# Six k-chunks cut 1, 2, 3, 3, 4, 3 in place of 1, 2, 2, 3, 4, 4, late transposes spread out, modulation sums two slots later

## The chip, the cores and the metric

The kernel runs on one core of a Trainium2 chip. The metric is device time in microseconds (us) of one launch. "PE" is the matmul engine, "PEld" its weight load, DVE the vector engine, ACT the scalar engine, POOL GpSimd, and SP the queue that issues nearly all DMAs.

## What is computed

One layer of a bidirectional hybrid encoder on 512 positions of width 2048, all in float32:

```python
mod = silu(c) @ w_ada + b_ada                  # (1, 6144)
shift, scale, gate = split(mod, 3)
h = rms_norm(x, g) * (1 + scale) + shift       # (512, 2048)
proj = h @ w_in                                # (512, 7168): q,k,v,z of 8 attention heads, q,k,v,z of 4 retention heads
y_a = dilated_attention_mixture(q_a, k_a, v_a) # three windows, ALiBi, mixed by their softmax denominators
y_r = bidirectional_retention(q_r, k_r, v_r)
y = concat(y_a * silu(z_a), y_r * silu(z_r))
out = rms_norm(x + gate * (y @ w_out), final_gain)
```

Keeping float32's accuracy, the kernel splits both operands of each large product into a high and a low part and issues three matmuls (`mm3`, L93 to L96: high·high, high·low, low·high).

## The kernel before, in words

The width 2048 is 16 tiles of 128, called k. `h` for a tile needs the modulation of that tile (128 columns of shift and 128 of scale, over all 2048 rows of `w_ada`), and the projection needs `h`. So the kernel starts the projection before all modulation is there. `CHUNKS` (L36) cuts the 16 tiles into six chunks. For each chunk the loop at the end of the first part (`for ci, nk in enumerate(CHUNKS)`) runs 13 units, each 256 columns of `w_in` (q, k, v, z of three pairs of attention heads, q of the fourth). Two units (`persist`) hold their sums in four PSUM banks over all chunks; the other 11 use three banks in turn (pool `psA`, tile `pw`), and after each chunk their partial sums are added into SBUF accumulators on DVE (L973, `acc<-acc,pw`; the first time ACT copies). A unit fills two banks, one half after the other, and a half can only begin when the bank of three halves before has been added. One unit per chunk, the last in order, is left in PSUM and goes on into the next chunk.

A unit of a chunk is cut into items of at most two k tiles: a chunk of 1 or 2 has 13 items, one of 3 has 26 (two tiles, then one), one of 4 has 26. An item has a load (SP), a conversion (`conv`: the high part on ACT, L178; the low part on DVE, L183) and its matmuls. `feed` keeps loads 8 items and conversions 2 items ahead of the matmuls, so matmuls run ten slots behind the feed. Chunks of 1 or 2 tiles share loads between units (`shared_conv`, 512 KB for two neighbouring units); larger ones load each unit by itself.

An `agenda` puts side work into the slots of the feed. `plan` spreads the pieces for the next chunk evenly over this chunk's items: `ada_pieces` gives loads of `w_ada` (SP, L230, tile `araw`, three buffers), products that accumulate 16 row tiles (L241 on DVE, `aacc<-araw,ct,aacc`; the first of the 16 is L237 on ACT), then `sums` (L271: PE transposes the accumulators into the one bank of pool `psM`; ACT reduces them with `junk`, L276; DVE adds the bias, L278 to L280), then `h_pieces` (ACT L195 and L200; DVE L209, `hl<-ht,hh`). For the first chunk `sums` is the short form at L255 to L261.

Side work too: `last_rows`, the transposes of the last 128 positions of x (L378, `psx`, through the same `psM` bank; DVE or ACT copies them out, L389). The four pieces stand in feed slots 10, 11, 12 and 13. In the second half of the last chunk the attention of finished heads runs between the items (`run_queue`, pieces separated by `None`, one group per item), and goes on through the units after it.

Which instruction of an engine stands where is decided by a scheduler from this program order.

Of the kernel before, what the change touches and what calls it, by code (L numbers as in the profile page):

```python
# [32 lines left out]
OFF_QA, OFF_KA, OFF_VA, OFF_ZA = 0, 1024, 2048, 3072  # L33
OFF_QR, OFF_KR, OFF_VR, OFF_ZR = 4096, 4608, 5120, 6144
UC = 256
CHUNKS = [1, 2, 2, 3, 4, 4]  # L36
N_PERSIST = 2
ADA_SPAN = 0.65
TAB_SPAN = 16
WARM = 4, 1, 1  # L40
FIRST_W = OFF_KA + UC
LAG = 3
RAW, RAW1, WB, LOOK, LEAD, LEAD0, LEAD1, EB, YB = 3, 3, 3, 2, 4, 2, 8, 1, 22


# [9 lines left out]
def trunk_kernel(ctx, tc, x, c, norm_gain, w_ada, b_ada, w_in, w_out, dec_f, dec_b, final_gain, out):  # L55
# [46 lines left out]

    groups = [range(sum(CHUNKS[:i]), sum(CHUNKS[: i + 1])) for i in range(len(CHUNKS))]
    xt_tiles = {i: hp.tile([P, len(g), S], F32, tag=f"g{i}", name=f"xT{i}") for i, g in enumerate(groups) if i}
# [108 lines left out]
    def h_pieces(k0, nk):  # L213
        return [(lambda f=f, k=k: f(k, nk, k0)) for f in (make_h, make_hl) for k in range(k0, k0 + nk)]

    def ada_pieces(k0, nk):
# [6 lines left out]
        def load(kr):  # L223
            raw = aap.tile([P, 2048], F32, tag="araw", name="araw", bufs=AR)
            rv = raw[:, : npc * 2 * n].rearrange("p (a b f) -> p a b f", a=npc, b=2)
            src = wa[kr * P : (kr + npc) * P, 0 : 2 * D].rearrange(
                "(a p) (b f) -> p a b f", p=P, b=2
            )[:, :, :, k0 * P : k0 * P + n]
            for b in range(2):
                nc.sync.dma_start(rv[:, :, b], src[:, :, b])  # L230
            raws[kr] = rv

        def add(kr):
            rv = raws[kr]
            for a in range(npc):
                if kr + a == 0:
                    first = nc.scalar.activation(acc[:, :, :n], rv[:, a], AF.Copy, scale=ct[:, 0:1])  # L237
                    if k0 in (1, 3):
                        after(first, marks["hh"])
                else:  # L240
                    ins = nc.vector.scalar_tensor_tensor(  # L241
                        acc[:, :, :n], rv[:, a], ct[:, kr + a : kr + a + 1], acc[:, :, :n],
                        op0=ALU.mult, op1=ALU.add,
                    )
                    if k0 in (1, 3) and kr + a == 1:
                        after(ins, marks["hl"])
# [37 lines left out]
        def step(i):  # L284
            if i >= AR:
                add(krs[i - AR])
            if i < len(krs):
                load(krs[i])

        return (  # L290
            [(lambda i=i: step(i)) for i in range(len(krs) + AR)]
            + [sums]
            + h_pieces(k0, nk)
        )
# [182 lines left out]
    def last_rows(b):  # L477
        if b == 1:
            v = xn[3][:, 1024:D]
            after(nc.vector.tensor_scalar_mul(v, v, rsx[:, 3:4]), marks["sc"])  # L480
        turned(3, b, True)
        evacuated(3, b, dve if b else act, True)

    late = [lambda b=b: last_rows(b) for b in range(4)]
# [429 lines left out]
    k0 = 0  # L914
    agenda = {}
    fed = 0

    for i, f in enumerate(late):
        agenda.setdefault(LEAD1 + LOOK + i, []).append(f)

    def plan(fs, start, span):
        for i, f in enumerate(fs):
            agenda.setdefault(start + (i * span) // len(fs), []).append(f)
# [14 lines left out]

    for ci, nk in enumerate(CHUNKS):
        lastc = ci == len(CHUNKS) - 1  # L940
        early["on"] = ci < len(CHUNKS) - 2
        items = []
        order = ORDER
        if (len(CHUNKS) - 1 - ci) % 2:
            order = order[::-1]
# [48 lines left out]
        if not lastc:  # L994
            n2 = CHUNKS[ci + 1]
            nxt = []
            for i in range(0, n2, 4):
                nxt += ada_pieces(k0 + nk + i, min(4, n2 - i))
            before_last = ci == len(CHUNKS) - 2
            span = int(len(items) * ADA_SPAN) if before_last else len(items)  # L1000
            plan(nxt, fed + LAG, span)
            if before_last:
                agenda.setdefault(fed + LAG + span, []).append(open_wk)
        if ci == 0:
# [358 lines left out]
```

## Time and profile before

| | |
|---|---|
| median of 3 runs | 942.23 us (941.79 to 944.12) |
| the profiled execution, its own time | 941.63 us |
| its span, first to last instruction | 939.9 us |
| granted TensorE clock over the span | 0.997 |
| PE / DVE / ACT busy over the span | 98% / 66% / 40% |

A matmul's row in the trace overlaps the next one's, since the engine is pipelined; how fast PE goes is read from the distance between starts, or from how many matmuls a stretch holds. Seen from PE, the first chunk begins at 25 us, the second at about 47, the third at about 86, the fourth at about 129, the fifth at about 185 and the last at about 258 us.

### The profile page before, as it was taken

What the parts mean: (1) busy time and instruction counts of PE and PEld (TensorE: products, weight loads), DVE (VectorE), ACT (ScalarE), POOL (GpSimd) and SP (SyncE); (2) the same over time, 40 slices, a digit from 0 to 9 for tenths busy, and PEclk for the clock granted to TensorE, in tenths of its full rate; (3) what the DMA queues carried; (4) which work ended last, traced back from release to release, by engine and by line L of the source; (5) the groups of instructions that cost most, each with busy time, mean ns of one, the idle gap of its engine ahead of it and who ended that gap; (6) DMA issues with size and microseconds to landing.
All of it is one profiled execution on the core that took longest, in us unless ns stands there. A gap on an engine that the chain in (4) does not pass through costs nothing.

```text
span 939.9 us, 14334 instructions
## 1 busy us (share of the span) xinstructions
PE 919.8 (98%) x5578; PEld 806.7 (86%) x5578; DVE 619.6 (66%) x1096; ACT 379.0 (40%) x747; POOL 12.5 (1%) x25
## 2 busy tenths in 40 slices
PE   8999899999999999999999999999999999999996
PEld 5787688888988888988998899998899988888896
DVE  4899999949557786666675565745644382547554
ACT  4843426253244655444443233422333372324321
POOL 2000000000000000000000000000000000000001
PEclk9999999999999999999999999999999999999998
DMA  9997798533332222214444534445523148244305
GB/s 329 352 311 245 253 318 298 175 94 113 107 96 68 68 68 68 68 46 135 146 146 141 179 107 154 140 126 165 163 64 113 59 160 297 90 125 143 109 5 180
DMA packets 110244, 141.50 MB, mean 151 GB/s; under 512 B 5800, under 2 KB 81496, under 8 KB 109792
## 3 DMA queue, kind: packets, MB, share of 16 engines
q1 hardware_dynamic: 109072, 137.27, 45.3%
q10 hardware_dynamic: 1008, 3.28, 0.9%
q8 instruction: 44, 0.72, 0.3%
q14 instruction: 24, 0.20, 0.1%
q0 software_dynamic: 96, 0.03, 0.0%
HBM read 136.36 MB, written 4.20 MB: 150 GB/s over the span
## 4 chain that ended last, share of the span: by engine, by line
PE 85%; DVE 7%; DMA 4%; issue 2%; ACT 1%; POOL 0%; SPq 0%; POOLq 0%; DVEq 0%; ACTq 0%
PE pp L96 24%; PE pp L94 12%; PE pw L96 12%; PE po L96 12%; PE pw L94 6%; PE po L94 6%; PE op L96 3%; DVE aacc L241 3%; DMA araw<-in_w_ada_dram 3%; PE sp L96 2%; PE op L94 2%; DVE acc L973 1%; PE tp L797 1%; DVE w L183 1%; DMA raw<-in_w_ada_dram 1%
## 5 line engine op out<-in xcount | busy, mean ns | idle before, releaser
L183 DVE TENSOR_TENSOR w<-raw,w 128x512 fp32r<-128x512 f32 (+1 forms) x288 | 193.1, 672 | 216.4 <-ACT w L178 214.0
L178 ACT CAST w<-raw 128x512 fp32r<-128x512 f32 (+1 forms) x289 | 174.8, 607 | 399.0 <-PE pp L96 187.6
L94 PE MATMUL pp<-w,hh 128*128 128x256 f32 x576 | 160.1, 278 | 0.0
L96 PE MATMUL pp<-w,hh 128*128 128x256 f32 x576 | 159.6, 277 | 0.0
L96 PE MATMUL pp<-w,hl 128*128 128x256 f32 x576 | 159.6, 277 | 0.0
L94 PEld LDWEIGHTS pp<-w,hh 128*128 128x128 f32 x576 | 108.2, 188 | 1.0 <-issue 0.3
L96 PEld LDWEIGHTS pp<-w,hh 128*128 128x128 f32 x576 | 108.2, 188 | 0.9
L96 PEld LDWEIGHTS pp<-w,hl 128*128 128x128 f32 x576 | 108.4, 188 | 0.0
L94 PE MATMUL pw<-hh,w 128*128 128x512 f32 x256 | 101.9, 399 | 4.3 <-DVE acc L973 3.5
L96 PE MATMUL pw<-hh,w 128*128 128x512 f32 x256 | 100.2, 392 | 0.4 <-DVE w L183 0.4
L94 PE MATMUL pp<-hh,w 128*128 128x512 f32 x256 | 99.7, 392 | 0.4 <-DVE kl L697 0.4
L96 PE MATMUL pp<-hl,w 128*128 128x512 f32 x256 | 100.0, 391 | 0.0
L96 PE MATMUL pp<-hh,w 128*128 128x512 f32 x256 | 99.9, 390 | 0.0
L96 PE MATMUL pw<-hl,w 128*128 128x512 f32 x256 | 99.6, 390 | 0.0
L96 PE MATMUL po<-w,yh 128*128 128x512 f32 (+1 forms) x252 | 91.0, 361 | 0.0
L94 PE MATMUL po<-w,yh 128*128 128x512 f32 (+1 forms) x252 | 91.0, 361 | 0.0
L96 PE MATMUL po<-w,yl 128*128 128x512 f32 (+1 forms) x252 | 91.0, 361 | 0.0
L241 DVE SCALAR_TENSOR_TENSOR aacc<-araw,ct,aacc 128x512 f32<-128x512 f32 (+2 forms) x75 | 76.0, 1014 | 5.8 <-ACT aacc L237 2.6
L973 DVE TENSOR_TENSOR acc<-acc,pw 128x512 f32<-128x512 f32 x100 | 66.5, 681 | 5.2 <-PE pw L96 4.8
L94 PEld LDWEIGHTS pw<-hh,w 128*128 128x128 f32 x256 | 48.0, 188 | 19.8 <-DVE acc L973 7.5
L96 PEld LDWEIGHTS pw<-hh,w 128*128 128x128 f32 x256 | 48.1, 188 | 10.9 <-DVE w L183 0.8
L94 PEld LDWEIGHTS pp<-hh,w 128*128 128x128 f32 x256 | 48.0, 188 | 10.8 <-DVE kl L697 0.8
(235 smaller groups left out, 1558.2 us busy)
## 6 DMA issues: line engine op xcount, KB each, us to landing
raw<-in_w_in_dram SPq DMA_DIRECT2D x94, 512.0 KB, 3.7
araw<-in_w_ada_dram SPq DMA_DIRECT2D x48, 512.0 KB, 6.2
graw<-in_w_ada_dram SPq DMA_DIRECT2D x64, 256.0 KB, 3.1
raw<-in_w_out_dram SPq DMA_DIRECT2D x32, 512.0 KB, 3.7
raw<-in_w_in_dram SPq DMA_DIRECT2D x16, 384.0 KB, 3.8
araw<-in_w_ada_dram SPq DMA_DIRECT2D x16, 384.0 KB, 4.0
res<-in_x_dram SPq DMA_DIRECT2D x16, 256.0 KB, 6.6
raw<-in_w_in_dram SPq DMA_DIRECT2D x11, 256.0 KB, 5.6
```

Of the source, the lines that this page charges most:

```text
L94: nc.tensor.matmul(o, lh, rh, start=start, stop=False, skip_group_check=True)
L96: nc.tensor.matmul(o, a, b, start=False, stop=stop and b is (rl if swap else rh), skip_group_check=True)
L178: c1 = nc.scalar.copy(dh, src)
L183: c2 = nc.vector.tensor_tensor(dl, src, f32(dh), op=ALU.subtract)
L241: ins = nc.vector.scalar_tensor_tensor(acc[:, :, :n], rv[:, a], ct[:, kr + a : kr + a + 1], acc[:, :, :n], op0=ALU.mult, op1=ALU.add,)
L797: nc.tensor.transpose(tp_[:, j * P : (j + 1) * P], pt[:, j * P : (j + 1) * P], ident)
L973: nc.vector.tensor_tensor(accs[u][i], accs[u][i], ps[i], op=ALU.add)
```

## The change

```diff
--- before.py
+++ after.py
@@ -33,13 +33,15 @@
 OFF_QA, OFF_KA, OFF_VA, OFF_ZA = 0, 1024, 2048, 3072
 OFF_QR, OFF_KR, OFF_VR, OFF_ZR = 4096, 4608, 5120, 6144
 UC = 256
-CHUNKS = [1, 2, 2, 3, 4, 4]
+CHUNKS = [1, 2, 3, 3, 4, 3]
 N_PERSIST = 2
 ADA_SPAN = 0.65
 TAB_SPAN = 16
 WARM = 4, 1, 1
 FIRST_W = OFF_KA + UC
 LAG = 3
+LATER = 2
+LATE = 10, 19, 23, 26
 RAW, RAW1, WB, LOOK, LEAD, LEAD0, LEAD1, EB, YB = 3, 3, 3, 2, 4, 2, 8, 1, 22
 
 
@@ -289,6 +291,7 @@
 
         return (
             [(lambda i=i: step(i)) for i in range(len(krs) + AR)]
+            + [lambda: None] * (LATER if k0 > 1 else 0)
             + [sums]
             + h_pieces(k0, nk)
         )
@@ -915,8 +918,8 @@
     agenda = {}
     fed = 0
 
-    for i, f in enumerate(late):
-        agenda.setdefault(LEAD1 + LOOK + i, []).append(f)
+    for at, f in zip(LATE, late):
+        agenda.setdefault(at, []).append(f)
 
     def plan(fs, start, span):
         for i, f in enumerate(fs):
```

The chunks now hold the tiles 0; 1, 2; 3 to 5; 6 to 8; 9 to 12; 13 to 15. Items: 13, 13, 26, 26, 26, 26 where there were 13, 13, 13, 26, 26, 26. The third chunk's weights are loaded unit by unit (13 loads of 384 KB) and no longer shared; the last chunk has items of two and of one tile in place of two and two. Two empty pieces stand ahead of `sums` in the side work for the third to the sixth chunk (the second's has none). The four pieces of `last_rows` go to slots 10, 19, 23 and 26. Below, lines of the changed kernel are numbered 2 or 3 higher: its L243 is L241 of before, L185 is L183, L976 is L973, L239 is L237, L278 is L276, L180 is L178.

DVE in the second chunk, around the end of the products for the third chunk's modulation (`aacc`), before; `acc_0` and `acc_1` are a unit's two halves, `md` holds the reduced sums:

```order
L183 TENSOR_TENSOR w<-raw,w 128x512
L241 SCALAR_TENSOR_TENSOR aacc<-araw,ct,aacc 128x2x256
L973 TENSOR_TENSOR acc_0_363<-acc_0_363,pw 128x512
L241 SCALAR_TENSOR_TENSOR aacc<-araw,ct,aacc 128x2x256
L973 TENSOR_TENSOR acc_1_364<-acc_1_364,pw 128x512
L241 SCALAR_TENSOR_TENSOR aacc<-araw,ct,aacc 128x2x256
L183 TENSOR_TENSOR w<-raw_610,w 128x512
L973 TENSOR_TENSOR acc_0_349<-acc_0_349,pw 128x512
L278 TENSOR_TENSOR sv<-md,bg 128x2
L973 TENSOR_TENSOR acc_1_350<-acc_1_350,pw 128x512
L183 TENSOR_TENSOR w<-raw,w 128x512
```

and now:

```order
L243 SCALAR_TENSOR_TENSOR aacc<-araw,ct,aacc 128x2x384
L976 TENSOR_TENSOR acc_1_373<-acc_1_373,pw 128x512
L243 SCALAR_TENSOR_TENSOR aacc<-araw,ct,aacc 128x2x384
L185 TENSOR_TENSOR w<-raw_621,w 128x512
L243 SCALAR_TENSOR_TENSOR aacc<-araw,ct,aacc 128x2x384
L976 TENSOR_TENSOR acc_0_358<-acc_0_358,pw 128x512
L243 SCALAR_TENSOR_TENSOR aacc<-araw,ct,aacc 128x2x384
L976 TENSOR_TENSOR acc_1_359<-acc_1_359,pw 128x512
L185 TENSOR_TENSOR w<-raw,w 128x512
L976 TENSOR_TENSOR acc_0_366<-acc_0_366,pw 128x512
L976 TENSOR_TENSOR acc_1_367<-acc_1_367,pw 128x512
L280 TENSOR_TENSOR sv<-md,bg 128x3
```

DVE's 15 products for that chunk (the sixteenth is ACT's) were of 2x256 columns and are of 2x384. The last of them stood behind the fourth of DVE's adds in this chunk and now stands behind the fifth; the adds that follow it are unchanged in kind.

ACT around the same sums, before (`junk` are the reductions, the product `aacc` ahead of them opens the chunk after):

```order
L178 CAST w<-raw 128x512 x2
L178 CAST w<-raw_610 128x512
L237 ACTIVATE aacc<-araw,ct 128x2x384
L178 CAST w<-raw 128x512
L276 ACTIVATE junk,md<-psm 128x128 x4
L178 CAST w<-raw 128x512
L195 ACTIVATE hh_79<-xT_93,sv,av 128x512
```

and now:

```order
L180 CAST w<-raw_621 128x512
L180 CAST w<-raw 128x512
L239 ACTIVATE aacc<-araw,ct 128x2x384
L278 ACTIVATE junk,md<-psm 128x128 x3
L180 CAST w<-raw 128x512
L278 ACTIVATE junk,md<-psm 128x128 x3
L180 CAST w<-raw_671 128x512
L197 ACTIVATE hh_79<-xT_93,sv,av 128x512
```

Six reductions in two groups in place of four, and the product that opens the chunk after stands directly ahead of the first of them.

DVE in the third chunk, about its middle, before:

```order
L241 SCALAR_TENSOR_TENSOR aacc<-araw,ct,aacc 128x2x384
L183 TENSOR_TENSOR w<-raw,w 128x512
L241 SCALAR_TENSOR_TENSOR aacc<-araw,ct,aacc 128x2x384
L973 TENSOR_TENSOR acc_0_367<-acc_0_367,pw 128x512
L973 TENSOR_TENSOR acc_1_368<-acc_1_368,pw 128x512
L241 SCALAR_TENSOR_TENSOR aacc<-araw,ct,aacc 128x2x384
L183 TENSOR_TENSOR w<-raw_747,w 128x512
L241 SCALAR_TENSOR_TENSOR aacc<-araw,ct,aacc 128x2x384
L973 TENSOR_TENSOR acc_0_353<-acc_0_353,pw 128x512
L973 TENSOR_TENSOR acc_1_354<-acc_1_354,pw 128x512
```

and now:

```order
L243 SCALAR_TENSOR_TENSOR aacc<-araw,ct,aacc 128x2x384
L185 TENSOR_TENSOR w<-raw_892,w 128x256
L243 SCALAR_TENSOR_TENSOR aacc<-araw,ct,aacc 128x2x384
L976 TENSOR_TENSOR acc_0_362<-acc_0_362,pw 128x512
L976 TENSOR_TENSOR acc_1_363<-acc_1_363,pw 128x512
L243 SCALAR_TENSOR_TENSOR aacc<-araw,ct,aacc 128x2x384
L185 TENSOR_TENSOR w<-raw,w 128x512
L243 SCALAR_TENSOR_TENSOR aacc<-araw,ct,aacc 128x2x384
L185 TENSOR_TENSOR w<-raw,w 128x256
L243 SCALAR_TENSOR_TENSOR aacc<-araw,ct,aacc 128x2x384
L976 TENSOR_TENSOR acc_0_376<-acc_0_376,pw 128x512
```

A unit's two adds had one low half and two products between them and the next unit's; now they have two low halves (512 and 256 columns) and two products, and PE has three tiles of matmuls for them where it had two.

## Rows read from the trace of the kernel before

**Rows 1.** The page: its first line, and busy time (share of the span, instructions) of each engine.

```profile
span 939.9 us, 14334 instructions
...
PE 919.8 (98%) x5578; PEld 806.7 (86%) x5578; DVE 619.6 (66%) x1096; ACT 379.0 (40%) x747; POOL 12.5 (1%) x25
```

**Rows 2.** Busy time of the engines in stretches of the span: from:to, length, then each engine's busy us with its instructions, granted TensorE clock, DMA share, GB/s.

```profile
70.00:114.00 44.00, 39.90 (x169) 30.05 (x168) 42.27 (x64) 17.71 (x36) 0.00 (x0) 1.00 0.81 262
80.00:114.00 34.00, 30.11 (x127) 22.25 (x126) 32.27 (x49) 13.14 (x29) 0.00 (x0) 1.00 0.85 278
161.00:205.00 44.00, 44.00 (x198) 35.94 (x197) 34.48 (x51) 12.47 (x35) 0.00 (x0) 1.00 0.46 146
145.00:161.00 16.00, 15.36 (x89) 12.68 (x88) 14.60 (x24) 11.36 (x31) 0.00 (x0) 1.00 0.92 310
44.00:50.00 6.00, 4.79 (x32) 3.89 (x31) 5.43 (x13) 2.75 (x4) 0.00 (x0) 1.00 1.08 357
```

**Rows 3.** PE's instructions in order of time: start, us, what. Two 512-column matmuls with 55 more between them, and two neighbours among the 256-column ones, of stretches in which PE never waits.

```profile
204.63 0.40 PE L94 MATMUL pw<-hh,w 128*128 128x512 f32 x1
...
217.35 0.39 PE L96 MATMUL pw<-hh,w 128*128 128x512 f32 x1
...
56.96 0.28 PE L94 MATMUL pw<-w,hh 128*128 128x256 f32 x1
57.08 0.28 PE L96 MATMUL pw<-w,hh 128*128 128x256 f32 x1
```

**Rows 4.** The same view, 44 to 156 us: the matmuls before which PE was idle (in brackets how long, and who ended it).

```profile
44.44 1.05 PE L255 MATMUL psm<-ones,aacc 128*128 128x1 f32 x8 [0.15 <-DVE aacc L241]
45.90 0.52 PE L378 MATMUL psx<-ident,xt 128*128 128x128 f32 x3 [0.41 <-DVE av L260]
47.07 0.66 PE L378 MATMUL psx<-ident,xt 128*128 128x128 f32 x4 [0.65 <-DVE xT L389]
...
64.20 0.50 PE L94 MATMUL pw<-hh,w 128*128 128x512 f32 x1 [0.77 <-DVE acc L973]
...
79.06 0.50 PE L94 MATMUL pw<-hh,w 128*128 128x512 f32 x1 [0.21 <-DVE acc L973]
82.71 0.50 PE L94 MATMUL pw<-hh,w 128*128 128x512 f32 x1 [0.62 <-DVE acc L973]
91.56 0.50 PE L94 MATMUL pw<-hh,w 128*128 128x512 f32 x1 [0.35 <-DVE acc L973]
96.14 0.50 PE L94 MATMUL pw<-hh,w 128*128 128x512 f32 x1 [1.34 <-DVE acc L973]
101.87 0.55 PE L271 MATMUL psm<-ident,aacc 128*128 128x128 f32 x3 [1.33 <-ACT junk L276]
...
152.11 0.50 PE L94 MATMUL pw<-hh,w 128*128 128x512 f32 x1 [0.21 <-DVE acc L973]
155.95 0.50 PE L96 MATMUL pw<-hh,w 128*128 128x512 f32 x1 [0.37 <-DVE w L183]
```

**Rows 5.** DVE's instructions in order of time, the same columns; L241 is a product for the modulation, L183 a weight's low half, L973 an add from PSUM, L209 a low half of the activations.

```profile
48.44 1.28 DVE L209 TENSOR_TENSOR hl<-ht,hh 128x512 fp32r<-128x512 f32 x2
...
60.28 0.74 DVE L241 SCALAR_TENSOR_TENSOR aacc<-araw,ct,aacc 128x512 f32<-128x512 f32 x1
60.94 0.68 DVE L973 TENSOR_TENSOR acc<-acc,pw 128x512 f32<-128x512 f32 x1
...
65.33 0.74 DVE L241 SCALAR_TENSOR_TENSOR aacc<-araw,ct,aacc 128x512 f32<-128x512 f32 x1
...
79.52 1.01 DVE L241 SCALAR_TENSOR_TENSOR aacc<-araw,ct,aacc 128x768 f32<-128x768 f32 x1
80.45 0.68 DVE L183 TENSOR_TENSOR w<-raw,w 128x512 fp32r<-128x512 f32 x1
81.05 1.01 DVE L241 SCALAR_TENSOR_TENSOR aacc<-araw,ct,aacc 128x768 f32<-128x768 f32 x1
81.98 1.28 DVE L973 TENSOR_TENSOR acc<-acc,pw 128x512 f32<-128x512 f32 x2
83.17 1.01 DVE L241 SCALAR_TENSOR_TENSOR aacc<-araw,ct,aacc 128x768 f32<-128x768 f32 x1
...
105.38 1.28 DVE L241 SCALAR_TENSOR_TENSOR aacc<-araw,ct,aacc 128x1024 f32<-128x1024 f32 x1
106.57 0.68 DVE L973 TENSOR_TENSOR acc<-acc,pw 128x512 f32<-128x512 f32 x1
```

**Rows 6.** ACT's instructions in order of time around the sums of two chunks: its own product (L237), which opens the next chunk, and the first `junk` reduction (L276) behind it.

```profile
63.68 0.94 ACT L237 ACTIVATE aacc<-araw,ct 128x768 f32<-128x768 f32 x1 [0.96 <-DMA araw<-in_w_ada_dram]
...
66.81 0.28 ACT L276 ACTIVATE junk<-psm 128x128 f32<-128x128 f32 x1 [0.29 <-PE psm L271]
...
99.89 1.15 ACT L237 ACTIVATE aacc<-araw,ct 128x1024 f32<-128x1024 f32 x1 [1.43 <-DMA araw<-in_w_ada_dram]
100.95 0.26 ACT L276 ACTIVATE junk<-psm 128x128 f32<-128x128 f32 x1
```

**Rows 7.** DMA issues from 20 to 120 us (count, KB each, median us from issue to landing), and what SP's queue waited for before it could issue modulation loads (0 to 420 us: total, times, longest).

```profile
araw<-in_w_ada_dram SPq DMA_DIRECT2D x25, 512.0 KB, 6.2
araw<-in_w_ada_dram SPq DMA_DIRECT2D x16, 384.0 KB, 4.0
...
SPq L230 <- DVE aacc L241: 39.9, 19, 6.2
```

**Rows 8.** The last chunk beside attention, 275 to 345 us: its row of the stretches; groups of DVE and PE instructions by shape (count, busy us, mean ns); and from 120 to 180 us the group of 256-column low halves.

```profile
275.00:345.00 70.00, 70.00 (x373) 59.16 (x372) 56.77 (x115) 40.22 (x78) 0.00 (x0) 1.00 0.22 70
...
L183 DVE TENSOR_TENSOR w<-raw,w 128x512 fp32r<-128x512 f32 x19 | 13.1, 690 | 8.0 <-ACT w L178 7.9
...
L94 PE MATMUL pw<-hh,w 128*128 128x512 f32 x59 | 23.3, 395 | 0.0
L94 PE MATMUL pw<-w,hh 128*128 128x256 f32 x32 | 9.0, 281 | 0.0
...
L183 DVE TENSOR_TENSOR w<-raw,w 128x256 fp32r<-128x256 f32 x13 | 5.4, 418 | 0.2 <-ACT w L178 0.2
```

## The prediction

> **What bounds the kernel now.** I read the page first, then the stretches, then PE's waits, then the engines that PE waits for. The page says that PE is busy 98% of a span of 939.9 us [rows 1]; the change moves neither a matmul out nor one in, apart from where they stand, so only lost PE time can be won or added. The stretches show where it is lost. From 161 to 205 us PE holds 198 matmuls in 44.0 us, one per 0.222 us; from 70 to 114 us, as long a stretch, it holds 169, six of them short transposes [rows 2]. Matmuls of 512 columns start 12.72/56 = 0.227 us apart, those of 256 about half that [rows 3] (a count includes the ones that the edges cut, so I compare counts with counts and price work by the distance). So one k tile of one unit, six of 512 or twelve of 256, takes 1.36 us of PE, and a chunk of n tiles 13 x 1.36 x n: 17.7, 35.4, 53.0 or 70.7 us. The granted clock is 1.00 in every one of these stretches, its upper level of 2.4 GHz, so the clock plays no part.
>
> PE's waits say who is late: from 64 to 96 us it is DVE's adds out of PSUM, at 101.87 us ACT's reductions for the fourth chunk, at 44 to 47 us the first sums and the late transposes, at 152 and 156 us DVE again [rows 4]. DVE is busy 42.27 of 44 us there [rows 2]. The starts of DVE's instructions give what each costs in its queue: a product 0.66 us at 512 columns, 0.93 at 768, 1.19 at 1024, a low half 0.60, an add 0.60 [rows 5]; a low half of 256 columns lasts 418 ns against 690 [rows 8], about 0.34 in the queue.
>
> From these, **DVE's load by chunk**. Third chunk before: 13 low halves 7.8, 20 adds 12.0, 15 products of 768 columns 14.0, three low halves of h 1.8, together 35.6 us against 35.4 of PE: every delay is PE's. Second chunk before: the same with products of 512 (9.9) and two low halves of h (1.2) plus about 1.3 of copies: 32.2 against 35.4.
>
> **The change, part by part.**
>
> *Chunk sizes, third chunk.* It now has 53.0 us of PE. DVE: 13 x (0.60 + 0.34) = 12.2, adds 12.0, products 14.0, lows 1.8: 40.0 us, 75%. The excess is gone. What it cost: from 80 to 114 us, 127 matmuls; 121 at 0.222 and six transposes at 0.11 are 27.5 of 34 us, so 6.5 lost [rows 2]. I leave 1.2, since the sums of the next chunk keep ACT's opening product ahead of the first reduction, the pattern that made PE wait 1.33 at 101.87 us [rows 4, 6]. Term: **-5.3** (ends -6.5, and -3.0 if its own adds and sums still make PE wait half as long).
>
> Here a page weighs in. By busy time PE was idle 34.0 - 30.11 = 3.9 us in that stretch, and with 3.9 in place of 6.5 the sum below would end 2.6 us higher. The Trainium skill ("Perfetto Trace Analysis", section Identifying the Most-Contended Engine) says that matmul busy time is no good measure, because matmuls are pipelined, and to take the busy share of the weight loads. By that rule the stretch has 22.25/34 = 65.4% against 35.94/44 = 81.7% at full pace, so 6.8 us are lost and the sum would end 0.3 us lower. The counts of the rows side with the rule.
>
> *Chunk sizes, second chunk.* Its next chunk has three tiles, so DVE's products grow from 9.9 to 14.0 and the lows of h from 1.2 to 1.8: 36.9 us against 35.4. The excess moves here, smaller and later filled. Step by step: the lows of h for this chunk end at 48.44 + 1.28 = 49.7 us, and before the last product ended at 65.33 + 0.66 = 66.0 [rows 5]. In the new order 15 products (14.0), five low halves (3.0), five adds (3.0) and copies (0.67) lie between: 70.3 us, 4.3 later. The sums stand behind 23 of the three z units' matmuls on PE where they stood behind 15, 1.8 us, less four transposes moved behind them (0.4): PE gets there 1.4 later. That leaves 2.9 us, of which PE's old wait of 0.77 at 64.20 us [rows 4], a wait in the same ring of three banks, is replaced. Of what is left, 2.1, part is paid back, since after the sums DVE's new order holds 11.5 us of work (eight adds, three low halves, two products, two copies, three lows of h) for about 18 us of PE until the third chunk begins, and the waits at 79 and 82 us (0.21, 0.62) fall away. Against this stands ACT's opening product for the fourth chunk, queued ahead of the reductions: its load can only be issued when the twelfth product has freed the buffer, and lands 4.0 us after issue [rows 7], about when PE asks; I add 0.7. 2.1 - 0.8 + 0.7 = 2.0. Term: **+2.0** (ends 0, where everything is filled, and +5.0, where this chunk loses what the third lost).
>
> *Late transposes spread and the first sums.* At 44 to 47 us PE is idle 0.15 + 0.41 + 0.65 = 1.2 us [rows 4], 4.79 of 6.0 busy [rows 2]. Fewer copies now stand between the sums and the lows of h. But DVE's order puts two more 512-column low halves (1.2 us) ahead of the last of the second chunk's products, so the sums start 1.2 us later, and four transposes that filled PE while it waited are gone from there. The lows of h come at about the same time, with 0.5 us less PE work done by then. Term: **+0.5** (ends -1.2, all idle time gone, and +1.2). The one piece that now stands behind the third chunk's sums shares their single bank; its four transposes and two copies (0.7 us of DVE) are in the count above.
>
> *Sums two slots later.* For the third chunk's sums this is in the 1.4 us above. For the later ones DVE's last product is far ahead of PE (75% load), so it moves nothing that ends last. Nothing, covered by that slack; without it each would be a wait like the 1.33.
>
> *Fourth chunk.* Before, 145 to 161 us, PE is idle 0.64 us [rows 2], 0.21 + 0.37 of it behind DVE [rows 4]; by the ratio of the other stretch (6.5 lost to 3.9 idle) that is 1.0. The fourth chunk's sums stand at the same place, but PE comes to them a tile's worth of the third chunk, 17.7 us, later, and DVE's products are only 15 x (0.93 - 0.66) = 4.0 later. Term: **-0.9** (ends 0 and -1.0).
>
> *Fifth chunk.* Four tiles as before, with products of 768 for the sixth in place of 1024: DVE's load falls. Nothing.
>
> *Last chunk.* Its weights shrink by a quarter while the attention that runs between its items stays per item. From 275 to 345 us, 177 matmuls of 512 columns and 96 of 256 (three times the groups shown) are 40.2 + 10.9 = 51.1 us; a quarter less leaves 57.2 of 70. DVE is busy 56.77 [rows 8]; 19 low halves (13.1) become pairs of 690 and 418 ns in place of 690 and 690, 2.6 less: 54.2 of 57.2, 95%, where it was 81%. Term: **+0.8** (ends 0, and +8, the rival below).
>
> Loads: 13 of 384 KB replace shared ones of 512 KB, and five more modulation DMAs come before 70 us; beside DVE's pace I see no queue that ends last, but see the second rival. The rest of the kernel is unchanged.
>
> **Sum**, against the profiled execution's 941.63 us: -5.3 + 2.0 + 0.5 - 0.9 + 0.8 = -2.9, so 938.7; that execution stands 0.6 under the median of the runs, 942.23. I forecast 938.8.
>
> **The rivals.**
>
> 1. *The second chunk's excess is filled* (terms +2.0 and +0.8 fall to 0): 941.6 - 5.7 = 935.9. For it: after the sums DVE has 11.5 us of work for 18 of PE. Against: the adds ahead of the sums stand behind more and longer products.
>
> 2. *The excess only moves.* The second chunk loses what the third lost: term +5.0 in place of +2.0, 941.7. For it: its load is 104% where the third's was 100%, and SP waited 39.9 us for DVE's products before it could issue modulation loads [rows 7]; three buffers, each with two products in place of four, make that a chain of 4.0 us landing plus DVE's turn. Against: 512 KB took 6.2 us to land and DVE still waited for little. That the two slots do nothing, since the plan has more pieces for the same 13 items, belongs here too.
>
> 3. *Slower: the last chunk becomes DVE's.* Place: 275 to 345 us of before. A DVE at 96% cost PE 7 us in the 44 from 70 to 114 us [rows 2]; at 95% over 57 us the same rate costs 9 in place of 0.8: 938.7 + 8.2 = 947. It decides from 6.3 us of lost PE time in that chunk (945.06). For it: the two numbers. Against: from 70 to 114 us PE waited for adds of one unit after another, while here low halves wait for ACT (8.0 us idle before them, rows 8), so DVE has room to work ahead.
>
> **How the numbers follow.** A measurement here can tell about 0.3% (2.8 us) from no change: faster is under 939.4, slower over 945.1. My forecast has 0.44, with its terms moving it between 936 and 942: 0.30 of that under 939.4, 0.14 within. Rival 1 has 0.20, faster. Rival 2 has 0.22: 0.20 within, 0.02 slower. Rival 3 has 0.14, slower. Faster 0.50, same 0.34, slower 0.16. The range, 934.5 to 944.5, leaves out rival 3 and the lowest end.
>
> **What would show it.** Right: 86 to 140 us without waits for adds, PE at 0.222 us per matmul; a wait of 1 to 3 us at the third chunk's sums near 70 us; attention in the last chunk with DVE over 90% busy and under 2 us of waits. Wrong: PE waiting for adds or for ACT's reductions by over 4 us between 50 and 90 us (rival 2), transposes or adds waiting for DVE by over 4 us between 270 and 340 us (rival 3), or new waits for low halves in the third chunk, whose items now alternate.

## The result and the profile after

The changed kernel takes **946.56 us** (median of 6 runs, 944.83 to 947.84) against 942.39 (6 runs, 940.68 to 944.12): 1.005 of the time before, interval 1.0038 to 1.0062. It is slower, by more than the 0.3% that a measurement can tell, and outside the range. Its profiled execution took 946.0 us, 4.4 more than the one of before [rows 1].

The page after, first line, busy time and granted clock in 40 slices:

```profile
span 944.2 us, 14400 instructions
...
PE 922.9 (98%) x5578; PEld 808.9 (86%) x5578; DVE 619.5 (66%) x1112; ACT 380.8 (40%) x769; POOL 12.5 (1%) x25
...
PEclk9989999999999999999999999999999999999998
```

PE has the same 5578 matmuls. DVE has 16 instructions more than in [rows 1], ACT 22. And there is an 8 in the third slice of the clock, 47 to 71 us, where I had written that the clock plays no part.

To place the 4.3 us of span I lined up the two PE streams: the start of a matmul, less the steady distances (0.227, 0.114 and 0.109 us by shape) of all matmuls ahead of it, is PE's lag. What the lag grows by in a stretch is what PE lost there, by waiting or at a lower clock. Worked out from all starts in both traces, the stretches being cut at the same amount of matmul work:

```
lag, us, at the end of the stretch                  before   after   after lost more by   term of the prediction
up to the last work of the first chunk                7.24    7.70     +0.46               -
the first sums (before: 44 to 50 us)                  9.51   14.33     +4.36               +0.5
second chunk                                         12.55   19.22     +1.85               +2.0
third chunk                                          18.56   20.01     -5.22               -5.3
fourth chunk                                         20.00   22.80     +1.35               -0.9
fifth chunk                                          20.92   23.65     -0.07                0
last chunk                                           22.65   26.72     +1.34               +0.8
the rest                                             27.83   31.96     +0.06                0
```

The stretches of after that answer to [rows 2] and to the first row of [rows 8] (94 to 138 us lies wholly in the third chunk, where 70 to 114 us of before began in the second):

```profile
94.00:138.00 44.00, 43.96 (x240) 37.18 (x239) 43.18 (x66) 17.54 (x40) 0.00 (x0) 1.00 0.93 306
44.00:50.00 6.00, 3.28 (x16) 2.36 (x15) 4.48 (x12) 1.83 (x4) 0.00 (x0) 0.80 0.98 320
275.00:345.00 70.00, 69.06 (x368) 58.01 (x368) 54.91 (x114) 39.08 (x79) 0.00 (x0) 1.00 0.24 72
```

The third chunk holds PE at full pace, as forecast: 43.96 of 44 us busy where before it was 39.90. At the first sums it is 3.28 of 6 in place of 4.79, at a clock of 0.80. PE's waits there and in the second chunk, after (they answer to [rows 4]):

```profile
46.97 1.36 PE L257 MATMUL psm<-ones,aacc 128*128 128x1 f32 x8 [2.23 <-DVE aacc L243]
48.74 0.87 PE L381 MATMUL psx<-ident,xt 128*128 128x128 f32 x3 [0.41 <-DVE av L262]
...
69.44 0.50 PE L96 MATMUL pw<-hh,w 128*128 128x512 f32 x1 [1.34 <-DVE acc L976]
74.02 0.50 PE L96 MATMUL pw<-hh,w 128*128 128x512 f32 x1 [1.34 <-DVE acc L976]
77.67 0.55 PE L273 MATMUL psm<-ident,aacc 128*128 128x128 f32 x3 [0.28 <-ACT junk L278]
```

The first sums waited 0.15 us before and now wait 2.23. PE's busy time and the clock around them, after, in steps of 2 us (PE busy, granted clock, DMA share, GB/s):

```profile
44.00:46.00 2.00, 0.74 (x4) 1.00 0.97 334
46.00:48.00 2.00, 1.03 (x8) 0.89 0.98 308
48.00:50.00 2.00, 1.51 (x6) 0.50 0.97 319
50.00:52.00 2.00, 2.00 (x7) 0.50 1.03 345
52.00:54.00 2.00, 2.00 (x8) 0.50 0.62 222
54.00:56.00 2.00, 2.00 (x10) 0.90 0.84 307
```

From just before 48 to about 54 us the clock is at 0.50, the lower level of 1.2 GHz; the stretch from 52 to 54 us holds 8 matmuls, busy throughout. In the kernel before every one of these steps is at 1.00.

Why the sums are late shows on ACT and DVE. The product that opens the modulation, then DVE's first and last product, after:

```profile
24.34 0.25 ACT L392 COPY xT<-psx 128x128 f32<-128x128 f32 x1
...
24.84 2.13 ACT L392 COPY xT<-psx 128x128 f32<-128x128 f32 x7
26.79 0.49 ACT L180 CAST w<-raw 128x256 fp32r<-128x256 f32 x1
27.09 1.16 ACT L974 COPY acc<-pw 128x512 f32<-128x512 f32 x2
...
28.57 2.33 ACT L974 COPY acc<-pw 128x512 f32<-128x512 f32 x4
30.79 0.73 ACT L239 ACTIVATE aacc<-araw,ct 128x512 f32<-128x512 f32 x1
```

```profile
31.55 0.75 DVE L243 SCALAR_TENSOR_TENSOR aacc<-araw,ct,aacc 128x512 f32<-128x512 f32 x1 [2.05 <-ACT aacc L239]
...
46.17 0.75 DVE L243 SCALAR_TENSOR_TENSOR aacc<-araw,ct,aacc 128x512 f32<-128x512 f32 x1
```

And before:

```profile
24.15 0.57 ACT L389 COPY xT<-psx 128x512 f32<-128x512 f32 x1
...
24.97 1.57 ACT L389 COPY xT<-psx 128x512 f32<-128x512 f32 x3
26.39 0.97 ACT L178 CAST w<-raw 128x256 fp32r<-128x256 f32 x2
27.23 2.27 ACT L971 COPY acc<-pw 128x512 f32<-128x512 f32 x4
29.47 0.72 ACT L237 ACTIVATE aacc<-araw,ct 128x512 f32<-128x512 f32 x1
```

The rows of L392 and L389 copy the same transposed tiles of x out of PSUM, in eight pieces after and in four before. `evacuated` (L385 after) cuts such a copy wherever a chunk border falls inside a group of transposes. The groups are 1-4, 5-7, 8-11 and 12-15 (`BANKS`). The old borders cut only the first of them, 5 copies a row tile; the new borders 3, 6, 9 and 13 cut all four, 8 copies. The pieces take little more time: 24.34 to 26.79 us, 2.45, in place of 24.15 to 26.39, 2.24 (a high half of h, 0.35, lies inside both). But the order of ACT's instructions came out different with them: six copies `acc<-pw` (2 and 4) stand ahead of the opening product, where four stood. It starts 1.32 us later; with the two low halves that the prediction had counted ahead of the last product (1.2 us), that product ends at 46.8 us in place of 44.3. The experiments will show that both parts of this delay come with the cut of the copies.

### The profile page after: what moved, and what is told of

It is laid out like the page before. It is cut to its first block, busy times and chain, and to the rows that moved or that the text cites. A ratio compares the mean times of both kernels' runs of the same rounds, so it can differ in the third digit from the quotient of the medians.

```text
span 944.2 us, 14400 instructions
## 1 busy us (share of the span) xinstructions
PE 922.9 (98%) x5578; PEld 808.9 (86%) x5578; DVE 619.5 (66%) x1112; ACT 380.8 (40%) x769; POOL 12.5 (1%) x25
## 3 DMA queue, kind: packets, MB, share of 16 engines
q10 hardware_dynamic: 1008, 3.28, 0.9%
## 4 chain that ended last, share of the span: by engine, by line
PE 83%; DVE 8%; DMA 4%; issue 2%; ACT 2%; POOL 0%; SPq 0%; POOLq 0%; DVEq 0%; ACTq 0%
PE pp L98 24%; PE pp L96 12%; PE pw L98 12%; PE po L98 12%; PE pw L96 6%; PE po L96 6%; PE op L98 3%; DVE aacc L243 3%; DMA araw<-in_w_ada_dram 3%; PE sp L98 2%; PE op L96 2%; DVE w L185 1%; PE tp L800 1%; DVE acc L976 1%; DMA raw<-in_w_ada_dram 1%
## 5 line engine op out<-in xcount | busy, mean ns | idle before, releaser
L185 DVE TENSOR_TENSOR w<-raw,w 128x512 fp32r<-128x512 f32 (+1 forms) x301 | 195.2, 650 | 220.5 <-ACT w L180 220.3
L180 ACT CAST w<-raw 128x512 fp32r<-128x512 f32 (+1 forms) x302 | 177.3, 589 | 398.6 <-PE pp L98 187.3
L243 DVE SCALAR_TENSOR_TENSOR aacc<-araw,ct,aacc 128x768 f32<-128x768 f32 (+2 forms) x75 | 76.1, 1014 | 7.2 <-DMA araw<-in_w_ada_dram 3.9
L976 DVE TENSOR_TENSOR acc<-acc,pw 128x512 f32<-128x512 f32 x100 | 66.3, 682 | 5.0 <-PE pw L98 4.8
L96 PEld LDWEIGHTS pw<-hh,w 128*128 128x128 f32 x256 | 48.1, 188 | 16.4 <-DVE acc L976 4.4
L98 PEld LDWEIGHTS pp<-hl,w 128*128 128x128 f32 x256 | 48.4, 189 | 10.0
```

What stands on the lines that cost most here:

```text
L96: nc.tensor.matmul(o, lh, rh, start=start, stop=False, skip_group_check=True)
L98: nc.tensor.matmul(o, a, b, start=False, stop=stop and b is (rl if swap else rh), skip_group_check=True)
L180: c1 = nc.scalar.copy(dh, src)
L185: c2 = nc.vector.tensor_tensor(dl, src, f32(dh), op=ALU.subtract)
L243: ins = nc.vector.scalar_tensor_tensor(acc[:, :, :n], rv[:, a], ct[:, kr + a : kr + a + 1], acc[:, :, :n], op0=ALU.mult, op1=ALU.add,)
L976: nc.vector.tensor_tensor(accs[u][i], accs[u][i], ps[i], op=ALU.add)
```

## The experiments

Differences in time below are ratios to runs of the kernel before on the same chip, so that kernels from different hours compare.

**1. The parts one by one.** `no_spread`: the changed kernel, transposes as before.

```diff
-LATE = 10, 19, 23, 26
+LATE = 10, 11, 12, 13
```

> The changed kernel with the late transposes back in slots 10 to 13 (chunks 1, 2, 3, 3, 4, 3 and the two later slots stay). Theory A (the new chunk borders cut the copies out of the transpose banks into more pieces, 9 more on ACT ahead of its opening product, so the first sums come late; PE waits 2.2 us at 47 us and its clock then stands at 0.5 for some 6 us): the wait stays, 945 to 947 us. Rival B (the late transposes were the work that filled PE at 44 to 48 us, and spreading them is what costs): 942 to 943 us, with the clock at 1.0 from 44 to 57 us.

Measured: 947.01 us, 1.0048 (1.0032 to 1.0065); 2.23 us of wait at 46.91.

`no_later`: the changed kernel, sums as before.

```diff
-LATER = 2
+LATER = 0
```

> The changed kernel without the two empty pieces ahead of the sums. Theory A: the first sums are untouched, 945.5 to 948 us; the third chunk's sums come a slot or two earlier on PE and wait 1 to 2 us longer near 75 us. If the two slots were what delays h for the third chunk, it would be 2 us faster than the changed kernel.

Measured: 946.27 us, 1.0045 (1.0028 to 1.0063); the wait 2.23 us again. The third chunk's sums do not come earlier on PE, and wait 0.88 us at 78 us, 0.6 longer than in the changed kernel where 1 to 2 were expected.

`chunks_only`: both of these edits, so the new chunks alone.

> Only the chunks 1, 2, 3, 3, 4, 3; late transposes in slots 10 to 13, sums not later. Theory A: the wait at the first sums and the half clock are there, 945 to 948 us; the third chunk loses 1 to 2 us where the kernel before lost 6. Rival B: 940 to 942.5 us.

Measured: 947.29 us, 1.0058 (1.0040 to 1.0077); the wait 2.23 us. PE's lag grows by 0.1 us in the third chunk, less than expected.

`old_chunks`: the old chunks, with the spread and the later sums.

```diff
-CHUNKS = [1, 2, 3, 3, 4, 3]
+CHUNKS = [1, 2, 2, 3, 4, 4]
```

> Chunks back to 1, 2, 2, 3, 4, 4, with the spread transposes and the later sums. Theory A: no extra copies, the wait at the first sums is 0.2 to 1.2 us and the clock stays at 1.0; 940.5 to 942.5 us. Rival B: the wait of 2 us and the half clock are still there, 945 to 946 us.

Measured: 947.99 us, 1.0062 (1.0046 to 1.0078). The first sums are as before (0.15 us of wait, clock 1.00), but the time is a plain miss of what I expected: PE loses 4 us more in the third chunk and 1 us more ahead of it.

So the wait of 2.23 us comes with the chunk borders in every kernel that has them, and neither with the spread nor with the sums. And these two parts, or one of them, cost over 5 us on the old chunks, where I had priced both near nothing; experiment 5 tells them apart.

**2. The copies.** `aligned`: the changed kernel with groups of transposes whose borders fit the chunks better, 6 copies a row tile.

```diff
-    BANKS = (1, 5), (5, 8), (8, 12), (12, 16)
+    BANKS = (1, 5), (5, 9), (9, 13), (13, 16)
...
-    scaled(0, P, 1024)
-    scaled(0, 1024, D)
+    scaled(0, P, 1152)
+    scaled(0, 1152, D)
```

(and so for row tiles 1 and 2)

> The changed kernel, with the groups of transposes cut at 1-4, 5-8, 9-12, 13-15 instead of 1-4, 5-7, 8-11, 12-15 (and the scaling of the rows cut at tile 9 instead of 8), so that a row tile leaves PSUM in 6 copies, not 8 (before: 5). Theory A, the extra copies on ACT hold the opening product back and with it the first sums: PE's wait ahead of the first sums falls from 2.23 us to under 0.6, the granted clock from 44 to 57 us is back at 1.00, PE's lag at 41 us of steady matmuls falls from 14.3 to 9.5 to 10, and the time to 941.5 to 943. Rival B, the second chunk's larger loads and adds hold them back whatever the copies do: wait 2.0 to 2.3 us, clock 0.75 to 0.87, time 946 to 947.

Measured: 943.86 us, 1.0018 (1.0006 to 1.0030), with the wait gone, in PE's rows:

```profile
44.77 1.05 PE L257 MATMUL psm<-ones,aacc 128*128 128x1 f32 x8 [0.15 <-DVE aacc L243]
46.23 0.63 PE L381 MATMUL psx<-ident,xt 128*128 128x128 f32 x4 [0.41 <-DVE av L262]
47.66 1.19 PE L96 MATMUL pp<-hh,w 128*128 128x512 f32 x4 [0.80 <-ACT hh L197]
```

The lag after the first sums is 10.09 us, 4.2 less than in the changed kernel, and the clock from 44 to 57 us 1.00. Theory A holds for the place; the time falls by 0.3% where 0.4 to 0.5 was expected, since the second chunk then loses 0.8 us and the third 1.6 more. DVE's order there has three low halves of 512 columns among the 15 products of the second chunk's modulation, as in the kernel before, and not the changed kernel's five.

`before_split`: the kernel before, its copies alone cut as the new borders would.

```diff
-                dst = xt_tiles[i][:, lo - g[0] : hi - g[0], t * P : (t + 1) * P]
-                src = psx[t, b][:, (lo - k0) * P : (hi - k0) * P].rearrange("p (k f) -> p k f", k=hi - lo)
-                marks[eng] = eng(dst, src)
...
+                cuts = [lo] + [q for q in (3, 6, 9, 13) if lo < q < hi] + [hi]
+                for lo, hi in zip(cuts, cuts[1:]):
+                    dst = xt_tiles[i][:, lo - g[0] : hi - g[0], t * P : (t + 1) * P]
+                    src = psx[t, b][:, (lo - k0) * P : (hi - k0) * P].rearrange("p (k f) -> p k f", k=hi - lo)
+                    marks[eng] = eng(dst, src)
...
```

> The kernel before, its chunks untouched, but each group of transposes copied out in the pieces that the new chunks would cut (borders at 3, 6, 9 and 13 too): 8 copies and more of a row tile instead of 5. Theory A: the opening product starts 1.3 us later, PE waits 2 to 2.3 us ahead of the first sums, the clock from 44 to 57 us falls to 0.75 to 0.90, and the time is 945.5 to 947.5. Rival B: the wait stays at 0.15 us and the time at 942 to 943.

Measured: 944.6 us, 1.0028 (1.0016 to 1.0040). ACT's opening product, and PE at the first sums:

```profile
28.35 2.33 ACT L973 COPY acc<-pw 128x512 f32<-128x512 f32 x4
30.58 0.73 ACT L237 ACTIVATE aacc<-araw,ct 128x512 f32<-128x512 f32 x1
```

```profile
46.76 1.05 PE L255 MATMUL psm<-ones,aacc 128*128 128x1 f32 x8 [2.23 <-DVE aacc L241]
```

With nothing changed but the cut, the product starts 1.1 us later, five low halves of 512 columns stand among DVE's 15 products in place of three, PE waits the same 2.23 us, and the clock from 44 to 57 us is 0.87. The lag after the sums is 3.5 us over the kernel before. The time is 1 us under what I expected, the mechanism is the expected one.

**3. The clock.** `fill`: three idle matmuls in the wait.

```diff
+FILL = 3
...
                 ps = bank(psM, "psm")
+                for _ in range(FILL):
+                    o = ps[:, 128:512].rearrange("p (a f) -> p a f", a=3)
+                    after(
+                        nc.tensor.matmul(o, ones, ident.unsqueeze(1).to_broadcast([P, 3, P]), start=True, stop=True),
+                        marks["add"],
+                    )
```

> The changed kernel with three idle matmuls (128 x 384, fp32, result never read) on PE between the last work of the first chunk and the first sums, where PE waited 2.23 us. Theory A, the wait costs twice, once as idle time and once as a granted clock that falls after it: the clock from 44 to 57 us is 0.97 or more instead of 0.74, the sums start at the same time, PE's lag at 41 us of steady matmuls falls by 1 to 2.5 us, and the time by 1 to 2.5 us to 944 to 945.5. Rival C, the clock follows from something else or what it costs is won back in the second chunk's waits for the products: time 946 to 947 either way; with the clock still under 0.9 the first, with the clock at 1.00 the second.

Measured: 945.84 us, 1.0038 (1.0024 to 1.0052). In the profile, which is the longest of its 12 executions (948.96 us), PE is busy through the old wait and the lag after the first sums is 13.3 us, 1.0 less than in the changed kernel; the clock falls all the same, 2 us later, after PE's next waits (for `av` and `hh`):

```profile
44.00:46.00 2.00, 2.00 (x8) 1.00 0.78 216
46.00:48.00 2.00, 1.58 (x10) 1.00 1.02 362
48.00:50.00 2.00, 1.29 (x6) 0.90 1.07 382
50.00:52.00 2.00, 2.00 (x9) 0.50 1.06 377
52.00:54.00 2.00, 2.00 (x8) 0.75 0.74 228
```

Its 12 executions divide: seven with a mean granted clock over the span of 0.997 or 0.998 have a median of 944.59 us, five with 0.995 or 0.996 one of 947.71. None of the changed kernel's six executions reached 0.997. This fits theory A, but does not show it: only the slowest execution left a trace, the mean over the span does not say where the clock fell, and the 12 executions of `before_split` divide without such a difference (944.11 us at 0.995, 944.61 at 0.997). By its median `fill` cannot be told from the changed kernel (1.0038 against 1.0050, intervals overlapping).

**4. The last chunk.** `aligned_last4`: as `aligned`, with a last chunk of four tiles.

```diff
-CHUNKS = [1, 2, 3, 3, 4, 3]
+CHUNKS = [1, 2, 3, 3, 3, 4]
...
-    BANKS = (1, 5), (5, 8), (8, 12), (12, 16)
+    BANKS = (1, 5), (5, 9), (9, 12), (12, 16)
```

> Chunks of 1, 2, 3, 3, 3, 4 tiles with groups of transposes cut at 1-4, 5-8, 9-11, 12-15 (6 copies of a row tile), sums two items later and late transposes spread as in the change. Theory A: first sums as in the kernel before (wait under 0.6 us, clock 1.00), the third chunk's 5 us won as in the change, and the last chunk of four tiles takes back the 1.2 us that one of three lost in the attention: 940 to 941.5, faster than both. Rival B: the first sums still wait over 2 us: 945 to 946. Rival D: the last chunk's 1024-column products, due in a shorter fifth chunk, hold DVE and PE up for 2 us or more at its start: 942 to 944.

Measured: 940.69 us, 0.9985 (0.9974 to 0.9997), the time that theory A had. The wait at the first sums is 0.16 us; the clock is a miss, for in the profile it fell after the next waits, to 0.87 from 44 to 57 us where 1.00 was expected. The last chunk and the attention beside it lose 1.7 us, as in the kernel before, and not 3.1.

**5. Which part costs 5 us on the old chunks.** `spread_only`: the kernel before with its late transposes spread.

```diff
+LATE = 10, 19, 23, 26
...
-    for i, f in enumerate(late):
-        agenda.setdefault(LEAD1 + LOOK + i, []).append(f)
+    for at, f in zip(LATE, late):
+        agenda.setdefault(at, []).append(f)
```

> The kernel before with its own chunks, and the late transposes at items 10, 19, 23, 26 instead of 10 to 13; the sums not moved. With the sums two items later as well these chunks lost 5.8 us, all of it in the third chunk. Theory J, the loss comes with the sums that are moved behind more adds: here the time is 942 to 943, the sums' wait in the third chunk 1.3 us as before. Rival K, it comes with the spread transposes, whose copies on DVE fall among the adds of the second and third chunk: 946 to 948.

Measured: 942.38 us, 0.9994 (0.9982 to 1.0006).

`later_only`: the kernel before with the sums two items later.

```diff
+LATER = 2
...
+            + [lambda: None] * (LATER if k0 > 1 else 0)
             + [sums]
```

> The kernel before with its own chunks, and the modulation sums two items later; the late transposes stay at items 10 to 13. Theory J: the loss of 5.8 us comes with the sums that are moved, 945.5 to 948, with waits of 2 us or more ahead of the sums or of accumulators between 90 and 105 us. Rival K: 942 to 943, and no such wait over 1.4 us. If both this kernel and that with the spread alone stay at 942 to 943, the two cost only together.

Measured: 948.17 us, 1.0050 (1.0033 to 1.0067). Theory J: the sums' move alone costs what both cost. PE's rows in the third chunk, then ACT's:

```profile
93.60 0.50 PE L96 MATMUL pw<-hh,w 128*128 128x512 f32 x1 [1.73 <-DVE acc L976]
97.58 0.55 PE L273 MATMUL psm<-ident,aacc 128*128 128x128 f32 x3 [0.75 <-DVE aacc L243]
102.57 0.55 PE L273 MATMUL psm<-ident,aacc 128*128 128x128 f32 x3 [2.50 <-ACT junk L278]
```

```profile
100.60 1.15 ACT L239 ACTIVATE aacc<-araw,ct 128x1024 f32<-128x1024 f32 x1 [4.69 <-DMA araw<-in_w_ada_dram]
101.66 0.26 ACT L278 ACTIVATE junk<-psm 128x128 f32<-128x128 f32 x1
```

ACT stands idle for 4.69 us before the product that opens the next chunk, where it stood 1.43 in [rows 6], but most of that difference is only a high half that no longer runs in between: the product starts 0.71 us later than before (100.60 against 99.89). What the move changes is PE's order. Two items later in the program, the sums' first transposes come 11 matmuls earlier on PE, which now gets there before DVE's last product and ACT's reductions are done: 0.75 and 2.50 us of wait in place of none and 1.33. And after these waits the clock falls, which it did not do in the kernel before (104 to 106 us, the columns of [rows 2]):

```profile
104.00:106.00 2.00, 2.00 (x6) 1.51 (x6) 1.40 (x4) 0.54 (x3) 0.00 (x0) 0.50 0.36 116
```

That the move costs this is shown by `later_only` and `spread_only`; how the 0.5% divides among order, load and clock is read from the trace and not tried.

**6. The two parts on the new chunks.** `last4_plain`: `aligned_last4` with neither.

```diff
-LATER = 2
-LATE = 10, 19, 23, 26
+LATER = 0
+LATE = 10, 11, 12, 13
```

> Chunks of 1, 2, 3, 3, 3, 4 tiles and the groups of transposes cut at 1-4, 5-8, 9-11, 12-15, but the late transposes at items 10 to 13 and the sums not moved, as in the kernel before. It tells what the spread and the later sums are worth where the copies no longer disturb the first sums. Theory E, they are worth little with these chunks: within 1.5 us of the 940.7 us that the same chunks gave with them. Rival F, they spare the end of the second chunk the four copies on DVE and the sums' wait: without them PE waits 2 us or more longer between 55 and 90 us, 942.5 to 944.

Measured: 944.56 us, 1.0016 (1.0002 to 1.0031): 0.3% over `aligned_last4`, so theory E does not hold.

`last4_no_later` (`LATER = 0` alone):

> Chunks of 1, 2, 3, 3, 3, 4 tiles, copies cut as in the version of 940.7 us, late transposes at items 10, 19, 23, 26, and the sums not moved. Theory L, the spread is what is worth 3.9 us, the sums' move nothing: 940 to 941.5. Rival M, the sums' move is what pays with these chunks, as the adds of the 768-column products are done by then: 943.5 to 945.

Measured: 941.85 us, 1.0000 (0.9987 to 1.0013).

`last4_no_spread` (`LATE = 10, 11, 12, 13` alone):

> Chunks of 1, 2, 3, 3, 3, 4 tiles, copies cut as in the version of 940.7 us, the sums two items later, and late transposes at items 10 to 13. Theory L, the spread pays: 943.5 to 945. Rival M, the sums' move pays: 940 to 941.5. If both kernels lie at 942 to 943, each brings half.

Measured: 941.6 us, 0.9998 (0.9986 to 1.0009). Neither L nor M: with these chunks each part brings about 0.15 to 0.2%, no more than the intervals leave open for one part alone, and together 0.3%, which is clear of them.

`last4_late`: `aligned_last4` with the last two transposes in the third chunk.

```diff
-LATE = 10, 19, 23, 26
+LATE = 10, 19, 44, 48
```

> Chunks of 1, 2, 3, 3, 3, 4 tiles and the groups of transposes cut at 1-4, 5-8, 9-11, 12-15, sums two items later, and the last two of the four late transposes (tiles 9 to 15, needed by the fifth chunk at the earliest) moved from items 23 and 26, in the second chunk, to 44 and 48, in the third. Theory G, DVE sets the second chunk: two 128x512 copies fewer there, at 0.6 us each, take 0.6 to 1.2 us from PE's waits for acc between 55 and 75 us (5.0 us in all between 40 and 170 us), and the third chunk, where PE waited for nothing, takes them beside its matmuls: 939.5 to 940.2. Rival H, the third chunk has no slack on DVE: the gain is given back there, 940.5 to 942.

Measured: **940.26 us, 0.9971 (0.9959 to 0.9983)**, the fastest of all; its interval overlaps that of `aligned_last4`, so the expected 0.4 to 1.2 us cannot be told. Its third chunk, the stretch that answers to [rows 2]:

```profile
94.00:138.00 44.00, 44.00 (x254) 38.44 (x253) 43.30 (x68) 17.60 (x40) 0.00 (x0) 1.00 0.86 277
```

`late_no_later`: the same with `LATER = 0`.

> The best version so far (chunks of 1, 2, 3, 3, 3, 4, transposes at items 10, 19, 44, 48), with the sums not moved. Theory L, nothing hangs on the sums' move: 939.5 to 941. With a cost of the move as with the old chunks, it would be faster than that version by 2 us or more, under 938.5. Rival M, the move pays: 942.5 to 944.5.

Measured: 941.87 us, 0.9997 (0.9986 to 1.0008), between the two expectations: the later sums are worth 0.26% there, and here the intervals do not overlap. The traces show a place. In the fifth chunk, 176 to 230 us of steady matmuls, PE's lag grows by 2.0 to 2.2 us in all three kernels on these chunks whose sums are not moved, and by 0.5 in the three where they are; in `late_no_later` PE waits 1.16 us for an add there, at 236.6 us, and in `last4_late` for nothing.

## Why the prediction was wrong

The forecast was 938.8, a sum of -2.9 us against the profiled execution; the traces show +4.3. The step that failed is **the late transposes and the first sums**, priced at +0.5 with bounds of -1.2 and +1.2 and measured at +4.4. It makes 3.9 of the 7 us between forecast and result. The fourth chunk makes 2.2 more, and 0.5 us were lost ahead of the first sums, where the sum had no term.

- *First sums.* The prediction followed DVE's queue back to its last product and found 1.2 us of low halves more, then held that the lows of h come at about the same time. They start 1.9 us later (50.38 us against 48.44 in [rows 5]). It did not follow the chain one step further back, to where that queue starts: ACT's opening product. The chunk sizes also set where the copies of transposed x are cut, three copies a row tile more, after which the product starts 1.32 us later. The two low halves belong to the same cause: `before_split` has them with the old chunks, and `aligned`, with the new chunks, has not. Cutting the copies alone puts 3.5 us of lag into the kernel before; aligning the groups takes 4.2 out of the changed one. That is shown; why the scheduler orders the engines' work differently with more copies was not looked into.
- *"The clock plays no part."* Wrong at the same place. It was read from a trace whose longest idle time there was 0.65 us [rows 4]; the new wait is followed by 6 us at half clock. Of the 4.4 us, 2.1 are the longer wait, 0.3 lie in the eight short matmuls of the sums (1.36 in place of 1.05 us) and about 2 in those that follow. This profile has the deepest fall: in the four other kernels with the same wait and no filler the clock is 0.87 from 44 to 57 us, not 0.74, and the stretch costs 3.0 to 3.5 us more than before. How much the lower clock adds to the whole time in the changed kernel is not settled, for its execution with the lowest mean clock (0.993, 946.0 us) was not its longest. The Trainium skill ("TensorE: Matmul & The Clock Gate", section What's actually happening) says of the warm-up at a kernel's start that the chip watches activity in a window that runs free of the program, and that the same kernel therefore differs from run to run. The executions of `fill` agree in that the mean clock differs, 0.995 to 0.998 for one program, and so do those of the kernel before: 25 at 0.998 with a median of 941.5 us, 24 at 0.996 with one of 943.7 (but eight at 0.995 with one of 942.8). That window itself is shown by no run here.
- *Third chunk*, -5.3: right in kind and size, -5.2. By the distances of the matmuls the kernel before loses 6.0 us there, near the 6.5 counted and not the 3.9 of idle time; after, PE waits for no add from 86 to 140 us, as forecast.
- *Second chunk*, +2.0: +1.9. The size is in part luck. The prediction had PE wait 2.9 us at the third chunk's sums for DVE's last product. PE comes to these sums at 75.28 us without waiting; it lost the time earlier, for adds (1.34 and 1.34 us), and 0.28 us at the reductions, which were to cost 0.7.
- *Sums two slots later*, nothing: in the changed kernel no difference can be told (1.0050 with them, 1.0045 without, intervals overlapping). But the price was no price: by itself the same move costs 0.5% on the old chunks, where PE comes to the sums 11 matmuls earlier and waits, and gains 0.15 to 0.26% on chunks of 1, 2, 3, 3, 3, 4. "Covered by slack" was not checked against the order that the move gives PE.
- *Fourth chunk*, -0.9: +1.35. The old idle time went, as said, but a new one came: DVE's products for the last chunk wait for their loads, ahead of the adds and low halves that PE needs:

```profile
155.51 2.07 DVE L243 SCALAR_TENSOR_TENSOR aacc<-araw,ct,aacc 128x768 f32<-128x768 f32 x2 [0.43 <-DMA araw<-in_w_ada_dram]
157.50 0.42 DVE L185 TENSOR_TENSOR w<-raw,w 128x256 fp32r<-128x256 f32 x1
159.88 1.02 DVE L243 SCALAR_TENSOR_TENSOR aacc<-araw,ct,aacc 128x768 f32<-128x768 f32 x1 [1.97 <-DMA araw<-in_w_ada_dram]
```

```profile
161.56 0.39 PE L98 MATMUL pw<-w,hh 128*128 128x256 f32 x1 [0.44 <-DVE w L185]
163.42 0.39 PE L96 MATMUL pw<-w,hh 128*128 128x256 f32 x1 [0.33 <-DVE acc L976]
168.47 0.38 PE L96 MATMUL pw<-w,hh 128*128 128x256 f32 x1 [0.69 <-DVE acc L976]
```

  This is read, not tried: no run took those loads out. Kernels with three tiles in the third and fourth chunk lost 1.6 to 4.5 us in that stretch of their profiles, the kernel before 1.4; what decides between them is open.
- *Last chunk*, +0.8: +1.3, and rival 3, with 9 us at the same place, did not come. Nor did the load behind it: from 275 to 332 us, the 57 us meant, DVE is busy 43.56 us, 76% and not 95%. That the loss comes with a last chunk of three tiles is shown by `aligned_last4`, where it is gone.

None of the rivals was the cause. The total came out near rival 3's 947 for another reason, by chance.

## What to carry to other kernels

When a constant that sets tile or chunk sizes changes, look for every other place that is cut by it, and count instructions per engine before and after: here eight small copies in place of four, 0.2 us of ACT's time, were enough to change what stands ahead of the first instruction of a chain. Follow a wait back to the instruction that starts the chain, not only through the queue that ends it. And a move "into slack" is priced only when the order that comes out of it is read on every engine: sums put two items later in the program came 11 matmuls earlier on PE, which cost 0.5% with one set of chunks, while the same two items gained 0.15 to 0.26% with another.

## What the runs showed of the hardware

- A fall of the clock to 0.50 follows idle time of PE, but not each such stretch alike. In `aligned` PE was busy 1.67 and 0.97 of 2 us from 44 to 48 us and the clock stayed at 1.00; in `aligned_last4` it was busy 1.54 and 1.10, and the clock went to 0.50 at 48 us:

```profile
44.00:46.00 2.00, 1.54 (x11) 1.00 1.04 364
46.00:48.00 2.00, 1.10 (x5) 0.85 0.87 314
48.00:50.00 2.00, 2.00 (x8) 0.50 1.04 347
```

  From 44 to 57 us all six profiles of kernels whose first sums come late (after, `no_spread`, `no_later`, `chunks_only`, `before_split`, `fill`) show a clock of 0.74 to 0.87. Of the other eleven, eight show 1.00 and three 0.87 (`aligned_last4`, `last4_plain`, `last4_late`).
- Executions of one program differ in the mean granted clock that they got, and in two programs the time goes with it: by 3.1 us between the two groups of `fill` and by 2.2 us between 0.998 and 0.996 in the kernel before. In `before_split` it does not. A single profile can show either, so the lags above, one profile a kernel, carry such a difference.
- Cutting copies out of PSUM into twice as many pieces, of one and of three tiles in place of four, cost ACT 0.2 us on 1.9 (2.10 against 1.89 us, after against before).
